# Hybrid two-layer kernel: DMA copies in halves, host-transposed x, 96-row gate matmuls, a new order of gates and outputs

## The chip, the cores and the metric

The kernel runs on one core of a Trainium2 chip. The metric is device time in microseconds, from the start of one execution to its end, median of several runs. The engines are TensorE (PE, with PEld for its weight loads), VectorE (DVE), ScalarE (ACT), GpSimd (POOL) and SyncE (SP), which issues most DMA transfers. Each of them runs its own list of instructions in order, and waits at an instruction until what that needs is there.

## The reference

A sequence of T = 256 tokens of width D = 1024 goes through two layers and a final norm, all in float32:

```python
h = rms_norm(x, norm_w)
proj = h @ w_in
(aq, ak, av, az, c_glu, cz, dq, dk, dvv, dz, db, da, gate_logits) = split(proj)
y_a = diff_attention_branch(aq, ak, av, az, ...)          # 8 heads, two softmaxes each, @ w_attn_out
y_c = conformer_conv_branch(c_glu, cz, ...)               # GLU, depthwise conv of 31 taps, layer norm, @ w_conv_out
y_d = gated_deltanet_branch(dq, dk, dvv, dz, db, da, ...) # below, @ w_dn_out
g_a, g_c, g_d = split(sigmoid(gate_logits), 3)
x = x + (g_a * y_a + g_c * y_c + g_d * y_d) @ w_out
```

The deltanet branch has 8 heads of 128 and works on blocks of time. Per block and head it solves a unit lower triangular system, whose matrix is made of key products and of a decay exp(g_i - g_j), g being a running sum of gates, and then a recurrence over blocks:

```python
g = cumsum(g)
decay = exp(where(causal, g[..., :, None] - g[..., None, :], -inf))
tri = where(strict, einsum('bhnid,bhnjd->bhnij', kb, k) * decay, 0) + eye(C)
sol = triangular_solve(tri, concat([v * beta, kb * exp(g)]), lower=True, unit_diagonal=True)
```

## The kernel before, in words

**Weights.** The weights are read once, as 288 chunks of 512 KB (`w_raw`, `load`, L420-424; three buffers). ACT rounds each chunk to a shorter float type (`w_hi`, a cast) and DVE subtracts (`w_lo`), so that one float32 product becomes three fast matmuls (`acc<-...`, L346): high by high, low by high, high by low. The activations are split likewise (`h_hi`, `h_lo`). Four chunks (two 128-row slices of the 1024 rows each) make a group of 512 output columns: 12 matmuls of 512 columns per chunk, or 24 of 256 where the output is wanted transposed. SP issues the load of chunk n+3 only when the `w_lo` of chunk n is done, since that frees its buffer.

**Order.** Nothing is scheduled by hardware. While the program is built, a planner (class `Stream`) keeps a clock for PE and one for each of ACT, DVE and POOL, and puts the steps of some dozens of generators ("streams") into the gaps beside the dense weight groups. A step is put into its engine's list when the planner's clocks say that its input is there. `dma(landing, ...)` (L353) lists a transfer on SP's queue and tells the planner in how many us it lands; `yield x` in a stream asks for a pause of x us. Once built, the order on each engine is fixed; a wrong guess becomes a wait.

**Stages of a layer.** `SEQ` (L58) is the order of the groups in the first part of a layer: v, k, q are deltanet's projections (0 and 1 are heads 0-3 and 4-7), t the position tables, z the output gates of deltanet, w, x the start of its recurrence with attention's values, c the conformer's projections, a attention's queries and keys, d the depthwise convolution (as matmuls with the shifted copies `u4` and the tap matrices `wd`). Then `PHASE` (L57) orders, for deltanet, conformer and attention, the gate groups (g0, g1, 512 columns of gate logits each) and the output groups (y0, y1, the branch's output times its matrix). `evac_gate` turns gate logits into gate tiles, `evac_y` multiplies them in. Last, w_out.

**Triangular solve** (`dn_keys`, L814 on), once for heads 0-3 and once for heads 4-7 in each layer. PE makes the decay exponents, four heads at a time in `psE`: three bf16 matmuls for each head (the parts `gp[0..2]` of the gates times the triangle `trib`) and one with the causal mask. The 16 x 16 diagonal blocks (`dn_vc`, 128 x 128) are written to device memory (`v_keep`), and one DMA reads them back with a broadcast, so that all partitions of a group of 16 have the same block: 8 source rows, 16 copies of each, 2048 floats per partition, 1 MB in all (`nrep`; `y_hi` for heads 0-3, `t` or `t8` for heads 4-7, after the buffers that it borrows). On these DVE does 15 steps (`dn_t` products, `dn_z` sums), each of which uses the sums before it. The recurrence follows with matmuls on `dn_r`, and its outputs are `o_d`.

**Start.** x is read as 256 KB quarters (`big<-in_x`), two by SP and two by ACT; PE transposes it 128 x 128 at a time into PSUM (`s<-cst,big`), ACT scales and rounds (`h_hi`), DVE takes the rest (`h_lo`), ACT squares for the norm. Eight matmuls on ones (L613) run before.

Of the kernel before, what the change touches and what calls it, by code (L numbers as in the profile page):

```python
# [19 lines left out]
P = 128  # L20
# [36 lines left out]
PHASE = {k: (("g", 0), ("y", 0), ("g", 1), ("y", 1)) for k in ("dn", "conv", "attn")}  # L57
SEQ = "v0 k0 t0 z0 k1 v1 q0 z1 w0 c0 x0 q1 a0 d1 w1 x1 c1 a1 d2".split()  # L58
TAPQ = 8
# [32 lines left out]
def kernel(  # L92
    ctx: ExitStack,
    tc: tile.TileContext,
    x: bass.AP,
    positions: bass.AP,
    wts: bass.AP,
# [109 lines left out]
    def load_x(src):  # L207
        xt = big()
        for q in range(2):
            for t in range(2):  # L210
                qs = slice(q * GW, (q + 1) * GW)
                (nc.sync, nc.scalar if src is x and first_x else nc.sync)[q].dma_start(
                    out=xt[:, t, qs], in_=src[t * P:(t + 1) * P, qs])
        first_x.clear()
        return xt

    first_x = [True]
    u4 = const.tile([P, 8, T], F32, name="u4")
# [3 lines left out]
    one = const.tile([P, 1], F32, name="one")  # L222
    nc.scalar.dma_start(out=cst[:, 0:CO_TRI], in_=consts[:, 0:CO_TRI])
    V.memset(ones, 1.0)
    for i in range(1, 4):
        G.memset(u4[32 * i:32 * i + 32, :, 0:i], 0.0)
    xt = load_x(x)
    S.activation(out=one, in_=ones[:, 0:1], func=AF.Square)
# [8 lines left out]
    pat = const.tile([P, PT_N], BF16, name="pat")  # L237
    trib, identb, mask_dn, mask_at = [pat[:, i * P:(i + 1) * P] for i in range(4)]
    ne16 = cst[:, CO_NE:CO_NE + 16]
# [372 lines left out]
    for _ in range(8):  # L612
        TE.matmul(out=idle[:, 0:P], lhsT=ones, rhs=ones, start=True, stop=True)  # L613
    clk[0] = 4.5
    st_n = start_norm()
    s_r = [(q, add(raw_half(xt, 0, st_n, q))) for q in range(2)]
    finish(s_r[0][1])
    prepare(2)
    prepare()

    for l in range(DEPTH):
# [80 lines left out]
        def ba_stream():  # L702
# [36 lines left out]
            g16 = gg.rearrange("p c h -> p (c h)")
            grem = sm.tile([P, 16], F32, name="grem", bufs=1)  # L740
            V.tensor_copy(out=gp[0], in_=g16)
            V.tensor_sub(out=grem, in0=g16, in1=gp[0])
            V.tensor_copy(out=gp[1], in_=grem)
            V.tensor_sub(out=gp[2], in0=grem, in1=gp[1])
# [784 lines left out]
def _patterns():  # L1529
# [62 lines left out]
```

## Time and profile before

| | us |
|---|---|
| Median of 3 runs | 1125.26 (1125.21 to 1127.08) |
| Profiled execution | 1127.93 |
| Its span in the trace | 1126.1 |
| PE busy | 1055.4 (94%) |
| DVE busy | 864.4 (77%) |
| ACT busy | 550.1 (49%) |

The mean granted clock of PE is 0.964 of full speed. The span is the time between the first and the last event of the trace; the 1.8 us between it and the execution's time lie around it. In the lines of the profile, a time line's row has the start, the duration, the engine, the line of the program, the operation and "output<-inputs"; in square brackets stands how long the engine was idle before it and what released it. A row of waits has the total, the number and the longest. A row of windows has the stretch, its length, the busy time of PE, PEld, DVE, ACT and POOL with the number of instructions, then the granted clock of PE, the share of DMA time and GB/s.

### The profile page before, as it was taken

To read this page: it belongs to the slowest core of one execution; us is meant where nothing else is said; L and a number is where in the kernel's file an instruction comes from. 1 tells how busy PE (TensorE), PEld (TensorE's weight loads), DVE (VectorE), ACT (ScalarE), POOL (GpSimd) and SP (SyncE) were. 2 spreads that over 40 slices of the span, in tenths; PEclk is the share of its full clock that TensorE was granted. 3 is DMA by queue.
4 is the path that set the end of the run, shared out by engine and by line. 5 is a ranking of instruction groups with operands and counts; after the bars stand their busy time and mean duration, and the time that the engine had idled before them with its cause. 6 is when DMAs were issued, how large, how long until landed. Compare 5 with 4: busy or idle time off the path is not lost.

```text
span 1126.1 us, 18152 instructions
## 1 busy us (share of the span) xinstructions
PE 1055.4 (94%) x6964; PEld 915.5 (81%) x6964; DVE 864.4 (77%) x1718; ACT 550.1 (49%) x981; POOL 105.5 (9%) x73
## 2 busy tenths in 40 slices
PE   7998798899999999999999969869999999999996
PEld 6987797689877787898888869758998768879885
DVE  5686887688677899985668869757787689889755
ACT  5663362426445556464465426314544545646543
POOL 0010110010020000121101111011001000011220
PEclk8999898989999999999999989979999999989999
DMA  6556555523634556565664564744354625646662
GB/s 211 155 166 160 161 178 147 128 101 112 181 119 127 181 158 203 174 200 187 198 188 150 167 155 131 224 116 131 95 154 146 168 76 173 197 137 190 199 200 82
DMA packets 57062, 178.07 MB, mean 158 GB/s; under 512 B 6288, under 2 KB 16144, under 8 KB 55696
## 3 DMA queue, kind: packets, MB, share of 16 engines
q1 hardware_dynamic: 55696, 175.43, 51.5%
q10 hardware_dynamic: 1280, 1.49, 0.4%
q8 instruction: 54, 0.88, 0.3%
q14 instruction: 32, 0.26, 0.1%
HBM read 172.44 MB, written 4.46 MB: 157 GB/s over the span
## 4 chain that ended last, share of the span: by engine, by line
PE 79%; DVE 10%; DMA 8%; ACT 1%; issue 1%; SPq 0%; ACTq 0%; DVEq 0%
PE acc L346 65%; PE s L344 11%; DVE w_lo L127 4%; PE s L351 3%; DMA y_hi<-v_keep 2%; DMA t<-v_keep 2%; DMA w_raw<-in_wts 2%; DVE big L127 2%; DMA v_keep<-dn_vc 1%; DVE dn_t L127 1%; ACT w_hi L127 1%; DMA big<-in_x 1%; DVE gx L127 0%; DVE y_lo L127 0%; DVE dn_z L127 0%
## 5 line engine op out<-in xcount | busy, mean ns | idle before, releaser
L127 ACT CAST w_hi<-w_raw 128x1024 fp32r<-128x1024 f32 (+1 forms) x289 | 302.2, 1047 | 363.3 <-PE acc L346 263.4
L127 DVE TENSOR_TENSOR w_lo<-w_raw,w_hi 128x1024 fp32r<-128x1024 f32 (+1 forms) x289 | 369.8, 1280 | 88.0 <-ACT w_hi L127 87.4
L346 PE MATMUL acc<-h_hi,w_lo 128*128 128x256 f32 x768 | 220.0, 286 | 21.0 <-DVE w_lo L127 21.0
L346 PE MATMUL acc<-h_hi,w_hi 128*128 128x256 f32 x768 | 226.9, 295 | 2.8 <-DVE dn_z L127 2.8
L346 PE MATMUL acc<-w_hi,h_hi 128*128 128x512 f32 x512 | 213.1, 416 | 6.6 <-ACT w_hi L127 6.6
L346 PE MATMUL acc<-h_lo,w_hi 128*128 128x256 f32 x768 | 219.3, 286 | 0.0
L346 PE MATMUL acc<-w_lo,h_hi 128*128 128x512 f32 x512 | 202.6, 396 | 1.9 <-DVE w_lo L127 1.9
L346 PE MATMUL acc<-w_hi,h_lo 128*128 128x512 f32 x512 | 202.4, 395 | 0.0
L346 PEld LDWEIGHTS acc<-h_hi,w_lo 128*128 128x128 f32 x768 | 149.1, 194 | 21.6 <-DVE w_lo L127 21.6
L346 PEld LDWEIGHTS acc<-h_hi,w_hi 128*128 128x128 f32 x768 | 149.4, 194 | 5.4 <-issue 4.8
L346 PEld LDWEIGHTS acc<-h_lo,w_hi 128*128 128x128 f32 x768 | 149.3, 194 | 0.5
L346 PEld LDWEIGHTS acc<-w_hi,h_hi 128*128 128x128 f32 x512 | 97.9, 191 | 25.4 <-ACT w_hi L127 7.5
L346 PEld LDWEIGHTS acc<-w_hi,h_lo 128*128 128x128 f32 x512 | 97.5, 190 | 21.4
L346 PEld LDWEIGHTS acc<-w_lo,h_hi 128*128 128x128 f32 x512 | 98.1, 192 | 20.1 <-DVE w_lo L127 3.5
L346 PE MATMUL acc<-w_hi,y_lo 128*128 128x512 f32 x128 | 52.1, 407 | 2.8 <-DVE y_lo L127 2.8
L127 DVE SCALAR_TENSOR_TENSOR c_acc<-c_u,pc,c_acc 128x255 f32<-128x255 f32 (+29 forms) x120 | 52.7, 485 | 2.6 <-ACT c_acc L127 2.6
L346 PE MATMUL acc<-w_hi,y_hi 128*128 128x512 f32 x128 | 53.2, 415 | 0.1
L346 PE MATMUL acc<-w_lo,y_hi 128*128 128x512 f32 x128 | 51.5, 402 | 0.0
L127 POOL TENSOR_TENSOR wa<-wa 128x512 f32<-128x512 f32 x16 | 23.8, 1490 | 281.4 <-DVE wa L127 235.5
L127 DVE SCALAR_TENSOR_TENSOR big<-wc,pc,big 128x255 f32<-128x255 f32 (+2 forms) x96 | 45.9, 519 | 0.0
L127 POOL TENSOR_TENSOR big<-big,gt 128x512 f32<-128x512 f32 x16 | 27.3, 1727 | 181.7 <-DVE gt L127 181.7
L346 PE MATMUL acc<-u,wd 128*32 128x256 f32 (+7 forms) x768 | 41.7, 369 | 1.2 <-ACT c_acc L127 1.2
(261 smaller groups left out, 1544.5 us busy)
## 6 DMA issues: line engine op xcount, KB each, us to landing
w_raw<-in_wts SPq DMA_DIRECT2D x288, 512.0 KB, 3.6
wd<-in_cwd SPq DMA_DIRECT2D x6, 1024.0 KB, 7.3
y_hi<-v_keep SPq DMA_DIRECT2D x2, 1024.0 KB
u_keep<-c_u SPq DMA_DIRECT2D x4, 512.0 KB, 5.2
t<-v_keep SPq DMA_DIRECT2D x2, 1024.0 KB
big<-in_x SPq DMA_DIRECT2D x6, 256.0 KB, 4.8
u<-u_keep SPq DMA_DIRECT2D x6, 256.0 KB, 4.0
u<-u_keep SPq DMA_DIRECT2D x6, 255.0 KB, 5.5
```

Of the source, the lines that this page charges most:

```text
L127: step = (self.key, lambda: getattr(self.eng, op)(*args, **kw), cost)
L344: live[0].steps.append(("PE", lambda: TE.matmul(**kw), cost))
L346: TE.matmul(**kw)
L351: ("PE", lambda: TE.transpose(out=out, in_=in_, identity=ident[0:n, 0:n]), 0.11))
```

## The change

1. x is also given transposed by the host, and layer 0 starts from it: four 256 KB pieces (three on ACT's queue, one on SP's), scaled and split without PE; the first weight chunk is loaded in two halves ahead of them on SP's queue. The squares are summed over rows by ACT and DVE later, and two matmuls of one column sum over partitions. The constants come in three pieces.
2. In `SEQ`, z1 moves from behind q0 to behind c1.
3. `PHASE` of deltanet and attention becomes g0 g1 y0 y1; the gate tiles of g1 come from the pool `wa`.
4. The decay exponents take one matmul per head instead of three: the running sums of the gates are made once per layer as rows (one 96 x 128 matmul), in three bf16 parts on 3 x 32 partitions (`crow`), and a 0/1 pattern `e3` of 96 rows picks the head and adds the parts.
5. The broadcast copy becomes two DMAs of 512 KB; new landings and pauses (3.5, 7.0 with 0.1, 8.0, and 6.0 ahead of the step that first needs the second half) go to the planner.

```diff
-SEQ = "v0 k0 t0 z0 k1 v1 q0 z1 w0 c0 x0 q1 a0 d1 w1 x1 c1 a1 d2".split()
+for k in ('dn', 'attn'):
+    PHASE[k] = (("g", 0), ("g", 1), ("y", 0), ("y", 1))
+SEQ = "v0 k0 t0 z0 k1 v1 q0 w0 c0 x0 q1 a0 d1 w1 x1 c1 z1 a1 d2".split()
...
-    xt = load_x(x)
+    xt = act.tile([P, KT, T], F32, name="big", bufs=3)
+    for k in (0, 2):
+        nc.scalar.dma_start(out=xt[:, k:k + 2], in_=x_t[:, k:k + 2])
...
+    def first_part(k):
+        sc = nwt[:, k:k + 1]
+        xh, xl = st_n["h"]
+        S.activation(out=xh[:, k, :], in_=xt[:, k, :], func=AF.Copy, scale=sc)
+        V.scalar_tensor_tensor(out=xl[:, k, :], in0=xt[:, k, :], scalar=sc, in1=xh[:, k, :].bitcast(F32),
+                               op0=ALU.mult, op1=ALU.subtract)
...
+    load()
+    nc.scalar.dma_start(out=xt[:, 4:6], in_=x_t[:, 4:6])
+    load()
+    nc.sync.dma_start(out=xt[:, 6:8], in_=x_t[:, 6:8])
+    load()
+    nc.scalar.dma_start(out=cst[:, 0:CO_NW], in_=consts[:, 0:CO_NW])
...
-    s_r = [(q, add(raw_half(xt, 0, st_n, q))) for q in range(2)]
-    finish(s_r[0][1])
+    for k in range(2):
+        first_part(k)
     prepare(2)
+    lows(0)
+    for k in range(2, 4):
+        first_part(k)
     prepare()
+    clk[0] = 6.5
+    s_f = add(first_half())
+    s_r = [(1, s_f)]
+    s_q = add(first_squares(), 0.1)
...
+            row = dn_tile()[0:96, 0:P]
+            mm(0.218, out=row, lhsT=gg.rearrange("p n a b -> p (n a b)"), rhs=tri, start=True, stop=True)
...
+            rem = sm.tile([P, P], F32, name="dn_t1", bufs=1)[0:96]
+            mid = sm.tile([96, P], BF16, name="crm", bufs=1)
+            V.tensor_copy(out=crow, in_=row)
+            V.tensor_sub(out=rem, in0=row, in1=crow)
+            V.tensor_copy(out=mid, in_=rem)
+            V.tensor_copy(out=crow[32:64], in_=mid[32:64])
+            V.tensor_sub(out=crow[64:96], in0=rem[64:96], in1=mid[64:96])
...
-                    for n in range(3):
-                        mm(0.055, out=psE[:, h * P:(h + 1) * P], lhsT=gp[n][:, j:j + 1].to_broadcast([P, P]),
-                           rhs=trib, start=(h == 0 and n == 0), stop=False)
+                    mm(0.055, out=psE[:, h * P:(h + 1) * P], lhsT=e3[:, j:j + 1].to_broadcast([96, P]),
+                       rhs=crow, start=(h == 0), stop=False)
...
-            dma(2.5, out=v_keep[hs], in_=vc.rearrange("p c h i -> p (c h i)"))
-            dma(
-                6.0, out=nrep.rearrange("p j c i -> p (j c i)"),
-                in_=v_keep[hs].rearrange("(b j) n -> b (j n)", b=8).unsqueeze(1).to_broadcast([8, 16, 16 * P]))
-            yield
+            dma(3.5, out=v_keep[hs], in_=vc.rearrange("p c h i -> p (c h i)"))
+            yield 3.5
+            for half in range(2):
+                dma(0.1 if half else 7.0, out=nrep[:, 8 * half:8 * half + 8].rearrange("p j c i -> p (j c i)"),
+                    in_=v_keep[hs].rearrange("(b h j) n -> h b (j n)", b=8, h=2)[half].unsqueeze(1).to_broadcast(
+                        [8, 16, 8 * P]))
+            yield 8.0
             z = sm.tile([P, 8, 16], F32, name="dn_z", bufs=1)
             V.tensor_copy(out=z, in_=bc_mid(eye16, 8))
...
-                if i % 3 == 0:
-                    yield
+                if i % 3 == 0 or i == 7:
+                    yield 6.0 if i == 7 else None
...
-                        g = flat(gt())
+                        g = flat(wa() if i else gt())
```

Two places show how the order moves. The first is SP's queue at the block copy of layer 0, heads 0-3 (`v_keep` written from `dn_vc`, then read back with the broadcast into `y_hi`). Before:

```order
L423 DMA w_raw<-in_wts 128x1024 x28
L354 DMA v_keep_85<-dn_vc 128x128
L354 DMA y_hi<-v_keep_85 128x1x2048
L423 DMA w_raw<-in_wts 128x1024 x15
L354 DMA u_keep<-c_u 128x4x256
```

After the change:

```order
L427 DMA w_raw<-in_wts 128x1024 x30
L357 DMA v_keep_85<-dn_vc 128x128
L427 DMA w_raw<-in_wts 128x1024 x4
L357 DMA y_hi<-v_keep_85 128x1x1024 x2
L427 DMA w_raw<-in_wts 128x1024 x4
L357 DMA u_keep<-c_u 128x4x256
```

Four weight loads moved between the write and the read, and the read is two DMAs, issued one right after the other.

The second place is DVE's list at the start of the solve on those blocks (`dn_z` set from the constants, then products `dn_t` and sums `dn_z`). Before:

```order
L127 COPY dn_z<-cst 128x128
L127 TENSOR_TENSOR w_lo<-w_raw,w_hi 128x1024
L127 TENSOR_TENSOR dn_t_1104<-dn_z,y_hi 128x8x2
L127 TENSOR_REDUCE dn_z<-dn_t_1104 128x8
L127 TENSOR_TENSOR dn_t_1105<-dn_z,y_hi 128x8x3
L127 TENSOR_REDUCE dn_z<-dn_t_1105 128x8
L127 TENSOR_TENSOR dn_t_1106<-dn_z,y_hi 128x8x4
L127 TENSOR_TENSOR w_lo<-w_raw,w_hi 128x1024
```

After the change:

```order
L130 TENSOR_TENSOR w_lo<-w_raw,w_hi 128x1024
L130 SCALAR_TENSOR_TENSOR vv<-wc,pc,vv 128x253
L130 COPY dn_z<-cst 128x128
L130 TENSOR_TENSOR dn_t_1372<-dn_z,y_hi 128x8x2
L130 TENSOR_REDUCE dn_z<-dn_t_1372 128x8
L130 TENSOR_TENSOR dn_t_1373<-dn_z,y_hi 128x8x3
L130 TENSOR_REDUCE dn_z<-dn_t_1373 128x8
L130 TENSOR_TENSOR dn_t_1374<-dn_z,y_hi 128x8x4
L130 TENSOR_REDUCE dn_z<-dn_t_1374 128x8
L130 TENSOR_TENSOR w_lo<-w_raw,w_hi 128x1024
```

The first read of `y_hi` stands behind a split of weights in both, one operation later than before; that split is the one which frees the buffer for the last of the four weight loads above (chunk 34 of 288, whose buffer chunk 37 takes). The next split follows after three steps of the solve.

More of the change, by code (lines that the diff above doesn't have):

```diff
@@ L95 @@
     x: bass.AP,
+    x_t: bass.AP,
     positions: bass.AP,
@@ L211, in load_x @@
                 qs = slice(q * GW, (q + 1) * GW)
-                (nc.sync, nc.scalar if src is x and first_x else nc.sync)[q].dma_start(
-                    out=xt[:, t, qs], in_=src[t * P:(t + 1) * P, qs])
-        first_x.clear()
+                nc.sync.dma_start(out=xt[:, t, qs], in_=src[t * P:(t + 1) * P, qs])
         return xt
-    first_x = [True]
     u4 = const.tile([P, 8, T], F32, name="u4")
@@ L222 @@
     one = const.tile([P, 1], F32, name="one")
-    nc.scalar.dma_start(out=cst[:, 0:CO_TRI], in_=consts[:, 0:CO_TRI])
+    nc.scalar.dma_start(out=cst[:, CO_NW:CO_TRI], in_=consts[:, CO_NW:CO_TRI])
     V.memset(ones, 1.0)
@@ L237 @@
     pat = const.tile([P, PT_N], BF16, name="pat")
-    trib, identb, mask_dn, mask_at = [pat[:, i * P:(i + 1) * P] for i in range(4)]
+    e3 = pat[0:96, 0:16]
+    identb, mask_dn, mask_at = [pat[:, i * P:(i + 1) * P] for i in range(1, 4)]
     ne16 = cst[:, CO_NE:CO_NE + 16]
@@ L422, in load @@
             raw = wpool.tile([P, KC, GW], F32, name="w_raw", bufs=RAW)
-            nc.sync.dma_start(out=raw, in_=wts[queue[len(raws)]])
+            for kk in range(KC) if not raws else [slice(0, KC)]:
+                nc.sync.dma_start(out=raw[:, kk], in_=wts[queue[len(raws)]][:, kk])
             raws.append((raw, clk[0] + 4.5))
@@ L604, in raw_half, with first_half, first_squares @@
             square_half(xt, st["ss"], q, t)
-    for _ in range(RAW):
-        load()
+    def first_part(k):
[4 more added lines that the diff above has]
+                               op0=ALU.mult, op1=ALU.subtract)
+    def first_half():
+        yield 1.5
+        for k in range(4, KT):
+            first_part(k)
+            yield
+    def first_squares():
+        yield from until(s_f)
+        sums = wc()[:, 0, :]
+        for q in range(2):
+            sq = wa().rearrange("p (a b) d -> p a (b d)", a=2)
+            sq2 = wa().rearrange("p (a b) d -> p a (b d)", a=2)
+            for n, s in enumerate((sq, sq2)):
+                S.activation(out=s, in_=xt[:, 4 * q + 2 * n:4 * q + 2 * n + 2, :], func=AF.Square)
+            yield
+            V.tensor_tensor(out=sq, in0=sq, in1=sq2, op=ALU.add)
+            V.tensor_tensor(out=sq[:, 0], in0=sq[:, 0], in1=sq[:, 1], op=ALU.add)
+            if q:
+                V.tensor_tensor(out=sums, in0=sums, in1=sq[:, 0], op=ALU.add)
+            else:
+                V.tensor_copy(out=sums, in_=sq[:, 0])
+            yield
+        pss = side_tile()
+        for t in range(2):
+            mm(0.218, out=pss[:, t:t + 1], lhsT=sums[:, t * P:(t + 1) * P], rhs=ones[:, 0:1],
+               start=(t == 0), stop=(t == 1))
+        ms = sm.tile([P, 2], F32, name="nms", bufs=2)
+        V.tensor_scalar(out=ms, in0=pss[:, 0:2], scalar1=1.0 / D, scalar2=1e-6, op0=ALU.mult, op1=ALU.add)
+        st_n["rn"] = rsqrt(ms, 2, "n")
+    load()
[4 more added lines that the diff above has]
+    nc.scalar.dma_start(out=cst[:, 0:CO_NW], in_=consts[:, 0:CO_NW])
     nc.scalar.dma_start(out=cst[:, CO_TRI:CO_N], in_=consts[:, CO_TRI:CO_N])
@@ L613 @@
         TE.matmul(out=idle[:, 0:P], lhsT=ones, rhs=ones, start=True, stop=True)
-    clk[0] = 4.5
+    clk[0] = 5.0
     st_n = start_norm()
-    s_r = [(q, add(raw_half(xt, 0, st_n, q))) for q in range(2)]
-    finish(s_r[0][1])
+    for k in range(2):
+        first_part(k)
     prepare(2)
+    lows(0)
+    for k in range(2, 4):
+        first_part(k)
     prepare()
+    clk[0] = 6.5
+    s_f = add(first_half())
+    s_r = [(1, s_f)]
+    s_q = add(first_squares(), 0.1)
     for l in range(DEPTH):
@@ L640 @@
         beta = lay.tile([P, 2, 8], F32, name="beta")
-        gg = lay.tile([P, 2, 8], F32, name="gg")
+        gg = lay.tile([P, 3, 2, 16], F32, name="gg")
         ng = lay.tile([P, 16], F32, name="ng")
@@ L679, in norm_stream @@
         def norm_stream():
-            yield from until(s_r[1][1])
-            st_n["rn"] = rn = inv_rms(st_n["ss"])
+            if l == 0:
+                yield from until(s_q)
+                rn = st_n["rn"]
+            else:
+                yield from until(s_r[1][1])
+                st_n["rn"] = rn = inv_rms(st_n["ss"])
             dgt = wa()
@@ L735, in ba_stream @@
             V.scalar_tensor_tensor(out=zl, in0=za, scalar=0.0, in1=zl, op0=ALU.max, op1=ALU.add)
-            V.scalar_tensor_tensor(out=gg, in0=zl, scalar=-1.0, in1=bc_mid(ea, 2), op0=ALU.mult, op1=ALU.mult)
+            V.memset(gg, 0.0)
+            g16 = gg[:, 0].rearrange("p a b -> p (a b)")[:, 0:16]
+            V.scalar_tensor_tensor(out=g16.rearrange("p (c h) -> p c h", c=2), in0=zl, scalar=-1.0,
+                                   in1=bc_mid(ea, 2), op0=ALU.mult, op1=ALU.mult)
+            V.tensor_copy(out=gg.rearrange("p n a b -> p n (a b)")[:, 1:3, 0:16], in_=bc_mid(g16, 2))
             yield
             psg = dn_tile()
[L739 to L744, printed above, removed]
             mm(0.218, out=psg[:, 0:16], lhsT=tri, rhs=g16, start=True, stop=False)
             mm(0.218, out=psg[:, 16:32], lhsT=ones, rhs=g16, start=False, stop=True)
+            row = dn_tile()[0:96, 0:P]
+            mm(0.218, out=row, lhsT=gg.rearrange("p n a b -> p (n a b)"), rhs=tri, start=True, stop=True)
             V.tensor_scalar(out=ng, in0=psg[:, 0:16], scalar1=-1.0, scalar2=None, op0=ALU.mult)
@@ L761, in evac_v @@
             return f
-        finish(s_r[0][1])
+        if l:
+            finish(s_r[0][1])
         s_norm = add(norm_stream(), 0.1)
@@ L810, in apply4 @@
             return pm
-        gp = [sm.tile([P, 16], BF16, name=f"gp{n}", bufs=1) for n in range(3)]
+        crow = lay.tile([96, P], BF16, name="crow")
         def dn_keys(hs, st):
@@ L1533, in _patterns @@
     c = np.zeros((P, PT_N), f)
-    c[:, 0:P] = p[:, None] <= p[None, :]
+    c[:, 0:16] = (p[:, None] % 32) == np.arange(16)[None, :]
     c[:, P:2 * P] = np.eye(P, dtype=f)
@@ L1576 @@
     arrays = {
-        "x": a["x"].reshape(T, D), "positions": a["positions"], "wts": wts, "wba": wba, "cwd": cwd,
+        "x": a["x"].reshape(T, D),
+        "x_t": a["x"].reshape(T, KT, P).transpose(2, 1, 0), "positions": a["positions"], "wts": wts, "wba": wba, "cwd": cwd,
         "pch": pch, "prow": prow,
```

## The prediction

> **What bounds the kernel now.** I read the page first (engines, slices), then the waits of PE and of DVE, then the time line of each long wait with the DMA of that stretch. The page's engine line:
>
> ```profile
> span 1126.1 us, 18152 instructions
> PE 1055.4 (94%) x6964; PEld 915.5 (81%) x6964; DVE 864.4 (77%) x1718; ACT 550.1 (49%) x981; POOL 105.5 (9%) x73
> ```
>
> TensorE (PE) has work 94% of the span, so the end moves in only two ways: PE waits less than 1126.1 - 1055.4 = 70.7 us, or it gets less work. The waits of PE, and of DVE (total, times, longest):
>
> ```profile
> PE acc L346 <- DVE w_lo L127: 22.9, 6, 10.5
> PE s L344 <- DVE dn_r L127: 16.5, 3, 10.6
> PE acc L346 <- DVE y_lo L127: 2.8, 2, 1.9
> PE s L351 <- DVE o_d L127: 1.9, 3, 1.1
> DVE dn_t L127 <- DMA y_hi<-v_keep: 25.0, 2, 13.0
> DVE dn_t L127 <- DMA t<-v_keep: 22.9, 2, 12.5
> ```
>
> Four waits of DVE for the block copy (y_hi or t from v_keep, 47.9 us together) stand behind PE's long ones. Here is the first (layer 0, heads 0-3):
>
> ```profile
> 99.58 0.43 SPq L354 DMA_DIRECT2D v_keep<-dn_vc  x1
> 102.54 1.22 DVE L127 TENSOR_TENSOR w_lo<-w_raw,w_hi 128x1024 fp32r<-128x1024 f32 x1
> 103.09 0.73 SPq L354 DMA_DIRECT2D y_hi<-v_keep  x1
> 116.77 0.19 DVE L127 TENSOR_TENSOR dn_t<-dn_z,y_hi 128x16 f32<-128x16 f32 x1 [13.01 <-DMA y_hi<-v_keep]
> 117.78 1.22 DVE L127 TENSOR_TENSOR w_lo<-w_raw,w_hi 128x1024 fp32r<-128x1024 f32 x1
> 119.05 0.58 PE L346 MATMUL acc<-h_hi,w_lo 128*128 128x256 f32 x1 [10.26 <-DVE w_lo L127]
> ```
>
> The copy lands 116.77 - 103.09 = 13.7 us after its issue. DVE works in order, so the next weight split (w_lo) is stuck behind the waiting read. PE had 13.01 + (119.05 - 116.77) - 10.26 = 5.0 us of work in hand and then stood still. After such a wait the granted clock is low too:
>
> ```profile
> 118.00:124.00 6.00, 4.95 (x23) 4.95 (x24) 5.76 (x14) 2.04 (x3) 0.00 (x0) 0.51 0.54 159
> ```
>
> A clock of 0.51 over 4.95 busy us costs another 2.4. [...]
>
> **The change part by part.** *Block copies.* SP no longer sits between v_keep and the copy; three or four weight loads stand there, and the copy goes in two halves. But the order puts DVE's first read of half 1 right behind the w_lo that frees the buffer of the last load ahead of it, so DVE again waits for a whole landing, now of one half. What does a half take? DMA shares in 40 slices of 98 to 120 us, and the same in GB/s:
>
> ```profile
> DMA  9302958710136299998995999564455344554001
> GB/s 380 142 0 22 179 223 341 264 44 0 30 60 89 89 201 179 223 194 149 194 171 74 186 216 171 75 112 104 134 119 112 67 112 171 201 216 186 7 0 7
> ```
>
> From about 111 us the copy is alone and keeps 4 to 5 tenths of the DMA engines busy. Size does not scale this away: v_keep, a sixteenth of the copy's bytes, lands 103.09 - 99.58 = 3.5 us after issue. With 3.3 fixed, a half takes 3.3 + 10.4/2 = 8.5, and 512 KB of weights issued just ahead go first: at the 341 of the row 1.5 us. So half 1 lands some 10.2 us after that w_lo ends, against 13.0 before. Bounds: 6.9 (half of 13.7, nothing fixed) and 13.7. I take 10.2, which is nearest to what the rows add up to. [...] Half 2 is read four or five weight chunks later and costs nothing, since 4 chunks of PE work (about 10.9 us, below) cover its 5.2.
>
> What hides 10.2 us? The 5.0 in hand, as before. The four places:
>
> ```profile
> 225.00 0.36 PE L346 MATMUL acc<-h_hi,w_hi 128*128 128x256 f32 x1 [2.81 <-DVE dn_z L127]
> 236.68 0.58 PE L344 MATMUL s<-dn_r,t 128*128 128x128 f32 x1 [2.60 <-DVE dn_r L127]
> 657.08 0.19 DVE L127 TENSOR_TENSOR dn_t<-dn_z,y_hi 128x16 f32<-128x16 f32 x1 [12.00 <-DMA y_hi<-v_keep]
> 660.07 0.58 PE L346 MATMUL acc<-h_hi,w_lo 128*128 128x256 f32 x1 [10.49 <-DVE w_lo L127]
> 751.97 2.07 PE L344 MATMUL s<-dn_r,dn_vo 128*128 128x128 f32 x8 [10.60 <-DVE dn_r L127]
> ```
>
> Layer 0, heads 0-3: 10.2 + 2.5 (three solve steps, 117.78 - 116.77 and a bit, then the split of 1.22) - 5.0 = 7.7 instead of 10.26: -2.6. Layer 1, heads 0-3: five steps now stand ahead of the next w_lo, as long as the 3.0 from 657.08 to 660.07 and 0.7 more: 10.2 + 3.7 - 4.7 = 9.2 instead of 10.49: -1.3. Layer 0, heads 4-7: today the depthwise matmuls hide most of the copy (2.81 + 2.60 are left). The change puts the solve among the conformer's projections, ahead of d2, and that cover is gone: 10.2 + 3.2 - 4.9 = 8.5, so +3.1. Layer 1, heads 4-7: 10.60 becomes 10.2 + about 3.5 (more steps, y_lo) - 4.9 = 8.8: -1.8. Sum -2.6; with less half clock behind the two shortened pairs I take -4. Bounds: -14 (landing 6.9) to +8 (landing 13.7 and no work in hand for heads 4-7).
>
> *SP behind u_keep.* In layer 1 SP stood on u_keep's landing, then w_raw came late:
>
> ```profile
> 709.80 0.44 SPq L354 DMA_DIRECT2D u_keep<-c_u  x1
> 710.29 0.50 SPq L354 DMA_DIRECT2D wd<-in_cwd  x1
> 715.26 1.93 SPq L354 DMA_DIRECT2D u<-u_keep  x4
> 727.75 0.56 PE L346 MATMUL acc<-w_hi,h_hi 128*128 128x512 f32 x1 [2.76 <-ACT w_hi L127]
> 729.01 0.80 PE L346 MATMUL acc<-w_lo,h_hi 128*128 128x512 f32 x1 [0.70 <-DVE w_lo L127]
> 729.00:735.00 6.00, 5.99 (x20) 5.22 (x21) 5.66 (x18) 1.39 (x2) 0.00 (x0) 0.51 0.47 146
> ```
>
> 715.26 - 709.80 = 5.5 us without a weight load, then 3.46 us of idle PE and 6 us at clock 0.51 (2.9 lost). The new order has a w_raw between u_keep and wd, so the stretch shrinks by one issue. Worth 0 to -6.4; I take -4.5.
>
> *Start.* Before (PE's transposes, h_hi, casts, first product):
>
> ```profile
> 5.62 0.39 ACTq L610 DMA_DIRECT2D pos_i<-in_positions  x1
> 7.90 2.61 PE L351 MATMUL s<-cst,big 128*128 128x128 f32 x11 [1.85 <-DMA big<-in_x]
> 8.83 2.55 ACT L127 ACTIVATE h_hi<-s,cst 128x256 fp32r<-128x256 f32 x6 [1.94 <-PE s L351]
> 13.72 3.02 ACT L127 CAST w_hi<-w_raw 128x512 fp32r<-128x512 f32 x4
> 14.38 0.79 PE L346 MATMUL acc<-w_hi,h_hi 128*128 128x512 f32 x1 [3.87 <-ACT w_hi L127]
> ```
>
> Now two h_hi and half a cast come ahead of the first product, on x as it lands: no transposes, and the squares move behind. ACT issues its pos_i load only when the second x piece is down (5.62 before; 5.6 to 7.9 now, 7.9 being the row of the last piece of x), then 2 x 2.55/6 = 0.85 and 3.02/4 = 0.75, and a hop: first product at 7.3 to 9.6, I take 8.0. That is -6.4; the two small matmuls of the norm give 0.4 back: -6.0, bounds -4.4 and -6.7. The squares, sums and low parts lie on ACT (49%) and DVE in the first 20 us, beside PE's first group.
>
> *Gate rows.* Twelve matmuls per block of four heads become four; before:
>
> ```profile
> 66.81 0.84 PE L344 MATMUL s<-pat,gp 128*128 128x128 bf16 x12
> 67.49 0.38 PE L344 MATMUL s<-pat 128*128 128x512 bf16 x1
> ```
>
> 67.49 - 66.81 = 0.68 for 12, 0.057 each. Two layers, two head sets, two blocks of time: eight such groups, 64 fewer matmuls, -3.6. The extra row matmul and the DVE operations (some 0.2 us each, like dn_t's 0.19, five more per layer) stand at the start of a layer, where PE has dense weight work in hand; if that cover failed it would be +1 per layer.
>
> *Phases g0 g1 y0 y1.* In layer 1 the first outputs wait for their inputs, deltanet's for o_d (1.9 in three waits, quoted above) just before 909 us and attention's for y_lo at 994.93:
>
> ```profile
> 909.00:913.00 4.00, 4.00 (x14) 3.15 (x13) 3.93 (x13) 0.59 (x2) 0.00 (x0) 0.58 0.02 4
> 994.93 0.79 PE L346 MATMUL acc<-w_hi,y_lo 128*128 128x512 f32 x1 [1.86 <-DVE y_lo L127]
> 998.00:1002.00 4.00, 4.00 (x12) 3.08 (x11) 1.28 (x2) 1.58 (x2) 0.00 (x0) 0.61 0.00 0
> 27.28 0.39 PE L346 MATMUL acc<-w_lo,h_hi 128*128 128x512 f32 x1
> 27.51 0.39 PE L346 MATMUL acc<-w_hi,h_lo 128*128 128x512 f32 x1
> ```
>
> A gate group ahead of y0 is 4 chunks of 12 products, 0.23 apart (the last two rows): 10.9 us for DVE to finish in. Waits of 1.9 and 1.9 go, with 4 x 0.42 = 1.7 and 4 x 0.39 = 1.6 of clock, and 0.9 that is left of y_lo's 2.8 in layer 0: at most -8.0. I take -6; it is 0 if the second gate tiles, now from another pool, hold up something else. z1's later place moves dense work only: 0.
>
> Sum: -4 - 4.5 - 6.0 - 3.6 - 6 = -24. The profiled execution took 1127.93 us (span 1126.1 and 1.8 around it), 2.7 above the median of 1125.26. Against the median: 1101 us.
>
> **The rivals.**
> 1. *The copies are hidden after all*: half 1 is down when DVE gets there. For it: v_keep's wait is gone, and a few loads more lie in between. Against: read and issue hang on the same w_lo. Remaining waits 10.26 + 10.49 + 10.60 + 5.4 = 36.7 go, with 2.4 of clock at three of them, instead of the 4 above: 1101 - 40 = 1061. It decides if DVE's waits for the copies sum to under 10 us.
> 2. *The change doesn't do what it says for the copies*: the pause meant for the landing moves the issue itself, and half 1, behind weights, comes as late as the whole (13.7). Then 3.5 more at each of four places, and half the phase and u_keep gains with it as the waits only wander: 1101 + 14 + 5 = 1120; with the other gains intact 1115.
> 3. *Slower*: for heads 4-7 the solve and the recurrence of heads 0-3 (dn_r) share DVE, and PE's next step hangs on dn_r. If the copy, all 15 steps and the recurrence run one after the other there (13.7, 15 steps at the 0.4 of 116.77 to 117.78, and four trips like the 2.60 above: 30), each layer stands 30 - 9 = 21 longer than forecast: 1101 + 42 = 1143. It decides from 12 us more per layer. Against it: chunks' splits stand between the steps in the order.
>
> **How the numbers follow.** Forecast 0.63, rival 1 0.09, rival 2 0.19, rival 3 0.09. Forecast's own ends: -14 and +8 of the copies, the u_keep and phase terms between full and none give 1087 to 1116. The range reaches down past this toward rival 1 and up over most of rival 2: 1084 to 1121. About 0.2%, 2.3 us, is what a measurement of this kernel can tell from no change. Faster: 0.63 + 0.09 + 0.15 = 0.87; same 0.03, the top of rival 2; slower 0.10.
>
> **What would show it.** Right: first product near 8 us; DVE's waits for the halves near 10 us each (7 for layer 0, heads 4-7), the w_raw ahead of them early; PE waits of 7 to 9 at four places; no w_hi wait after u_keep; no o_d or y_lo waits. Wrong: waits for the copies under 3 us, or a new releaser with over 10 us, first of all dn_r.

## The result, and the profile after

The changed kernel takes 1117.51 us (median of 4 runs, 1114.95 to 1120.10), the kernel before in the same measurement 1126.17: ratio 0.9921, 95% interval 0.9893 to 0.9949. It is faster by 8.7 us; the prediction said 24 (1101 us, range 1084 to 1121). The time lies in the range, the gain is a third of the forecast. The profiled execution took 1114.95 us, 12.98 less than the one before (1127.93).

The head of the page of the changed kernel:

```profile
span 1113.2 us, 18028 instructions
PE 1044.5 (94%) x6892; PEld 905.1 (81%) x6892; DVE 866.7 (78%) x1729; ACT 548.3 (49%) x977; POOL 102.3 (9%) x73
```

PE is idle for 1113.2 - 1044.5 = 68.7 us, against 70.7 before. So nearly all of the gain in this execution is busy time (1055.4 - 1044.5 = 10.9), and the waits have only changed places. Most of the busy time that went was work: PE's transposes of x (in the profile's groups `s<-cst,big` falls from 18.7 to 14.8 us) and the gate rows (`s<-pat,gp`, 6.8 us, became `s<-crow,pat`, 3.2). The rest goes with the clock, whose mean is 0.971 instead of 0.964. How the waits changed places, the waits of PE and of DVE say (total, times, longest):

```profile
PE acc L349 <- DVE w_lo L130: 14.7, 6, 6.7
PE s L354 <- POOL t L130: 11.7, 1, 11.7
PE s L347 <- DVE y_lo L130: 8.3, 2, 4.3
PE s L347 <- DVE gf L130: 6.3, 2, 3.5
DVE dn_t L130 <- DMA y_hi<-v_keep: 17.0, 2, 8.7
DVE dn_t L130 <- DMA t<-v_keep: 11.7, 2, 6.0
```

DVE waits 28.7 us for the copies instead of 47.9. The row `s <- POOL t` is new, and it is PE's longest wait. Two stretches of the time line belong to these rows. The first is the block copy of layer 0, heads 0-3:

```profile
109.12 0.42 SPq L357 DMA_DIRECT2D v_keep<-dn_vc  x1
119.79 1.35 SPq L357 DMA_DIRECT2D y_hi<-v_keep  x2
128.66 0.19 DVE L130 TENSOR_TENSOR dn_t<-dn_z,y_hi 128x16 f32<-128x16 f32 x1 [8.75 <-DMA y_hi<-v_keep]
131.17 0.58 PE L349 MATMUL acc<-h_hi,w_lo 128*128 128x256 f32 x1 [6.69 <-DVE w_lo L130]
```

The halves are issued 119.79 - 109.12 = 10.7 us behind the write of v_keep. Half 1 lands 128.66 - 119.79 = 8.9 us after its issue, and the reader arrives at once: DVE stands 8.75 us, PE 6.69. The second stretch comes 20 us later, where SP copies the conformer's activations:

```profile
139.23 0.43 SPq L357 DMA_DIRECT2D u_keep<-c_u  x1
139.71 0.51 SPq L357 DMA_DIRECT2D wd<-in_cwd  x1
144.53 2.16 SPq L357 DMA_DIRECT2D u<-u_keep  x4
146.79 0.40 SPq L427 DMA_DIRECT2D w_raw<-in_wts  x1
157.85 1.04 ACT L130 CAST w_hi<-w_raw 128x1024 fp32r<-128x1024 f32 x1 [12.03 <-DMA w_raw<-in_wts]
161.55 2.41 POOL L130 TENSOR_TENSOR t<-dn_z,cst 128x512 f32<-128x512 f32 x2 [68.34 <-DVE dn_z L130]
162.82 1.12 PE L354 MATMUL s<-cst,t 128*128 128x128 f32 x4 [11.65 <-POOL t L130]
169.27 1.01 PE L347 MATMUL s<-dn_vo,gf 128*128 128x128 f32 x3 [2.77 <-DVE gf L130]
```

No weights are requested from 139.2 to 146.8, then 2 MB (tap matrices and shifted copies) are ahead of them, and the chunk is there at 157.85, 11 us after its issue. ACT stands 12.03 us. Its cast is followed on DVE by the split, and behind that split lie the last two steps of the solve, which POOL's `t` and so PE's next matmul need. That is why the releaser reads POOL, an engine that had nothing to do with the cause. The granted clock of the stretch, with the fields of a window (length, busy PE, PEld, DVE, ACT, POOL, clock, DMA share, GB/s):

```profile
150.00:176.00 26.00, 11.57 (x40) 8.97 (x39) 13.80 (x24) 8.77 (x15) 2.41 (x2) 0.61 0.41 115
```

In 26 us PE is busy for 11.57, and that mostly at half clock (0.61 in the mean). Before the change the same copies also came without a load of weights between them (160.57 to 168.59), and the chunk behind them was there 9.7 us after its issue (178.31), but PE had products in hand until 182.9 us and waited only 3.3 (the rest of dn_r's 16.5 beside the 10.6 and 2.6 that the prediction quotes).

The start, in which ACT's wait for the DMAs shows:

```profile
9.38 0.39 ACTq L655 DMA_DIRECT2D pos_i<-in_positions  x1
9.82 0.91 ACT L130 ACTIVATE h_hi<-big,cst 128x256 fp32r<-128x256 f32 x2 [6.17 <-DMA big<-in_x_t]
11.29 0.80 PE L349 MATMUL acc<-w_hi,h_hi 128*128 128x512 f32 x1 [6.59 <-ACT w_hi L130]
```

The first product comes at 11.29 (14.38 before, 8.0 forecast).

### The profile page after: what moved, and what is told of

It is laid out like the page before. It is cut to its first block, busy times and chain, and to the rows that moved or that the text cites. A ratio compares the mean times of both kernels' runs of the same rounds, so it can differ in the third digit from the quotient of the medians.

```text
span 1113.2 us, 18028 instructions
## 1 busy us (share of the span) xinstructions
PE 1044.5 (94%) x6892; PEld 905.1 (81%) x6892; DVE 866.7 (78%) x1729; ACT 548.3 (49%) x977; POOL 102.3 (9%) x73
## 4 chain that ended last, share of the span: by engine, by line
PE 69%; DVE 17%; DMA 8%; issue 3%; ACT 2%; SPq 0%; ACTq 0%; DVEq 0%
PE acc L349 55%; PE s L347 11%; DVE w_lo L130 6%; DMA w_raw<-in_wts 4%; PE s L354 3%; DVE big L130 2%; DMA y_hi<-v_keep 1%; DMA t<-v_keep 1%; ACT w_hi L130 1%; DVE c_acc L130 1%; DVE vv L130 1%; DVE gx L130 1%; DMA big<-in_x_t 1%; DVE dn_t L130 1%; DMA u_keep<-c_u 0%
## 5 line engine op out<-in xcount | busy, mean ns | idle before, releaser
L130 DVE TENSOR_TENSOR w_lo<-w_raw,w_hi 128x1024 fp32r<-128x1024 f32 (+1 forms) x289 | 365.5, 1266 | 77.7 <-ACT w_hi L130 76.8
L349 PE MATMUL acc<-h_hi,w_hi 128*128 128x256 f32 x768 | 224.5, 292 | 0.0
L349 PE MATMUL acc<-w_hi,h_hi 128*128 128x512 f32 x512 | 216.0, 422 | 6.6 <-ACT w_hi L130 6.6
L349 PE MATMUL acc<-w_hi,t 128*128 128x512 f32 x128 | 40.0, 389 | 0.0
L349 PEld LDWEIGHTS acc<-u,wd 128*32 128x32 f32 x768 | 23.7, 110 | 18.3 <-ACT c_acc L130 3.5
```

The costliest lines, as they stand in the source:

```text
L130: step = (self.key, lambda: getattr(self.eng, op)(*args, **kw), cost)
L349: TE.matmul(**kw)
```

## The experiments

"Ratio" is to the kernel before, measured beside each kernel on the same chip, with its 95% interval. Three chips were used (e1 to e4, e5 to e8, e9 to e12), so kernels of different groups are best compared by their ratios.

| kernel | us | ratio |
|---|---|---|
| the change | 1117.51 | 0.9921 [0.9893, 0.9949] |
| e1 the change, z1 back | 1114.04 | 0.9891 [0.9872, 0.9911] |
| e2 the change, tap matrices earlier | 1110.82 | 0.9856 [0.9832, 0.9880] |
| e3 the change, halves issued early, read late | 1091.69 | 0.9686 [0.9662, 0.9710] |
| e4 the change, constants behind first scalings | 1112.37 | 0.9867 [0.9846, 0.9888] |
| e5 the change, old phases | 1117.56 | 0.9943 [0.9921, 0.9965] |
| e6 e3 with 16 source rows | 1080.82 | 0.9606 [0.9588, 0.9624] |
| e7 e6 with e4's start | 1079.84 | 0.9594 [0.9575, 0.9613] |
| e8 before, halves alone | 1120.63 | 0.9959 [0.9946, 0.9971] |
| e9 before, start and gate rows alone | 1131.08 | 1.0061 [1.0043, 1.0079] |
| e10 before, 16 source rows alone | 1104.22 | 0.9830 [0.9808, 0.9851] |
| e11 e7 with tap matrices far ahead | 1070.92 | 0.9528 [0.9508, 0.9548] |
| e12 before, halves and new phases | 1114.22 | 0.9920 [0.9898, 0.9941] |

**e1: z1 back behind q0.**

```diff
-SEQ = "v0 k0 t0 z0 k1 v1 q0 w0 c0 x0 q1 a0 d1 w1 x1 c1 z1 a1 d2".split()
+SEQ = "v0 k0 t0 z0 k1 v1 q0 z1 w0 c0 x0 q1 a0 d1 w1 x1 c1 a1 d2".split()
```

> The changed kernel with z1 back behind q0, nothing else. Theory A: what ate the gain is the wait of 11.7 us at 162.8 us and the half clock up to 175 us in layer 0, because z1's move brought u_keep, the tap matrices and the shifted copies (2.5 MB in one burst) to a place where only two weight chunks were ready. With z1 back u_keep comes four chunks later with a weight load behind it, that wait goes, and 10 to 18 us of the changed kernel's time with it: 1100 to 1108. Rival B: z1's place is neutral, as the prediction had it, and the wait at 162.8 us is the late end of the triangular solve, which is late here too: 1114 to 1120, the wait still there.

The wait at 162.8 us is gone, as A has it, and the time fell by only about 3 us, near B's end. SP's queue with z1 back:

```profile
149.64 0.43 SPq L357 DMA_DIRECT2D u_keep<-c_u  x1
152.05 0.34 SPq L427 DMA_DIRECT2D w_raw<-in_wts  x1
152.45 0.45 SPq L357 DMA_DIRECT2D wd<-in_cwd  x1
```

One load of weights goes between, and no PE wait over 0.5 us follows from 131 to 235 us. But others appear, in PE's waits of the same kernel:

```profile
PE s L354 <- ACT gx L130: 6.1, 1, 6.1
PE s L354 <- DVE big L130: 4.4, 2, 4.0
```

The recurrence of heads 4-7 (gx at 268 us) and attention's output (big at 987 us) now wait. PE's idle time falls from 68.7 to 1110.3 - 1050.0 = 60.3 us, but its busy time, for as many matmuls, rises from 1044.5 to 1050.0: part of the gain is lost in slower products. A's mechanism holds and its price doesn't: z1's four chunks of dense work hide something wherever they stand, and moving them bares something else.

**e2: tap matrices earlier.**

```diff
+            if s == 0 and NV < 2:
+                s_cv[NV] = add(conv_load(NV))
             s_g = group_a(l, ("in", CG + s * GW), H, evac_g)
...
-                if s == 0 and NV < 2:
-                    s_cv[NV] = add(conv_load(NV))
```

> The changed kernel with the 1 MB of tap matrices loaded ahead of the conformer's first group (nine loads of weights sooner in layer 0) and no longer between u_keep and the shifted copies; order of DVE and PE unchanged. Theory A (the burst holds back weight chunk 42): the chunk lands some 2.5 to 5 us sooner, the wait at 162.8 us falls from 11.7 to 6 to 9, time 1109 to 1114. Rival B (the solve ends late by itself): wait and time unchanged, 1115 to 1119.

ACT's and PE's rows at the same place:

```profile
152.48 1.04 ACT L130 CAST w_hi<-w_raw 128x1024 fp32r<-128x1024 f32 x1 [5.56 <-DMA w_raw<-in_wts]
157.45 0.90 PE L354 MATMUL s<-cst,t 128*128 128x128 f32 x3 [5.19 <-POOL t L130]
```

With 1 MB less ahead of it the chunk is there 152.48 - 146.27 = 6.2 us after its issue instead of 11.1, and PE's wait falls from 11.65 to 5.19. The order on DVE and PE is the same, so the burst, not a late solve, sets this wait; A stands, its time (1109 to 1114) too. How long it is varies with the execution (7.2 us in e4's, 9.8 in e5's, which leave the burst alone).

**e3: halves issued early, read placed behind the landing.**

```diff
             dma(3.5, out=v_keep[hs], in_=vc.rearrange("p c h i -> p (c h i)"))
-            yield 3.5
+            yield
             for half in range(2):
-                dma(0.1 if half else 7.0, out=nrep[:, 8 * half:8 * half + 8].rearrange("p j c i -> p (j c i)"),
+                dma(9.0 if half else 0.1, out=nrep[:, 8 * half:8 * half + 8].rearrange("p j c i -> p (j c i)"),
...
-            yield 8.0
+            yield 3.5
```

> The changed kernel with the pauses where they act: the halves are issued 3.5 us after the write of v_keep instead of 11.5, and DVE's first step of the solve is placed 9 us behind their issue. Theory C (in the changed kernel the 8.0 pause holds back the issue of the halves instead of the read): DVE's waits for the copies fall from 28.7 us to under 6, PE's four waits behind them (6.7, 4.0, 6.5, 4.3) go, and with the half clock behind them 20 to 30 us: 1088 to 1098. Rival D (the halves share the DMA engines with the weight loads, so whatever is not waited for at the copy is waited for at the next weight chunk): waits move to the casts and splits of weights, 1108 to 1117.

The issue of the first copy, then PE's and DVE's waits:

```profile
107.42 0.43 SPq L357 DMA_DIRECT2D v_keep<-dn_vc  x1
113.64 1.74 SPq L357 DMA_DIRECT2D y_hi<-v_keep  x2
PE acc L349 <- ACT w_hi L130: 15.6, 3, 6.0
PE acc L349 <- DVE w_lo L130: 3.2, 6, 0.9
DVE dn_t L130 <- DMA y_hi<-v_keep: 3.8, 2, 2.3
DVE dn_t L130 <- DMA t<-v_keep: 0.4, 1, 0.4
```

C holds. A pause given by `yield` is added to the planner's time before the steps just listed are placed, so the change's 8.0 held back the copies themselves, in the planner's time 3.5 + 8.0 = 11.5 us behind v_keep, while the read followed the issue at once. By the same rule the `yield 3.5` left in e3 puts the halves 7.0 us behind v_keep and not 3.5, as was expected. In the traces they come 5.1 to 9.2 us behind it at the four places (here 113.64 - 107.42 = 6.2), in the changed kernel 10.5 to 11.2. With that, and the read placed 9 us behind the issue, the waits for the copies fall from 28.7 to 4.2 us, and about 25 us go. Not all of that is the copies': the new order also puts a load of weights between u_keep and the tap matrices (at 141.12 us), and PE's wait for POOL's `t` is 1.8 us instead of 11.7. D is there too, but small: of the 15.6 us for casts, 4.7 (at 130.0 us) and 4.8 (at 656.6) are weight loads stuck behind the copies.

**e4: constants behind the first scalings.** The four loads of `cst`, `cst`, `pat` and `pos_i` on ACT's queue stand behind `prepare(2)` and `lows(0)`.

> The changed kernel with the four loads of constants, patterns and positions on ACT's queue moved behind the first two scalings and the first cast. Theory E (ACT stands at the issue of these loads while the first two pieces of x are there): scaling starts at 7.4 us instead of 9.8, the first product at 9 instead of 11.3, 2 to 2.5 us faster than the changed kernel: 1114 to 1116. Rival F (x or the first half of the weights lands that late): first product at 11 to 11.5, time unchanged.

```profile
7.04 0.51 ACT L130 ACTIVATE h_hi<-big,cst 128x256 fp32r<-128x256 f32 x1 [3.38 <-DMA big<-in_x_t]
8.50 0.50 PE L349 MATMUL acc<-w_hi,h_hi 128*128 128x512 f32 x1 [3.66 <-ACT w_hi L130]
```

E holds: the first piece of x was there at 7.0, ACT stood at an issue that waited for another piece (pos_i, at 9.38 in the changed kernel). The first product gains 11.29 - 8.50 = 2.8; the time gains 5, more than E said, and a shorter wait at 157.9 us (7.2 instead of 11.7 in the profiled executions) is large enough for the rest.

**e5: old phases.**

```diff
-for k in ('dn', 'attn'):
-    PHASE[k] = (("g", 0), ("g", 1), ("y", 0), ("y", 1))
...
-                        g = flat(wa() if i else gt())
+                        g = flat(gt())
```

> The changed kernel with the phases of deltanet and attention back at g0 y0 g1 y1 and the second gate tiles back in their pool. Theory H (the prediction's term): the new order of phases is worth 6 us, so this kernel takes 1122 to 1126, with waits for o_d and y_lo at layer 1's outputs of about 3.8 us and half clock behind them. Rival I: only the waits for o_d (1.9) and layer 0's y_lo (0.9) went with it, since attention's wait of 1.9 for y_lo at 995.6 us is still there in the changed kernel: 2 to 4 us, 1118.5 to 1121.5.

1117.56 against 1117.51: by the medians neither H nor I, and the phases are worth nothing here. By the ratios (0.9943 against 0.9921) they are worth 2.5 us, with intervals that overlap, so I isn't excluded. H's waits did not come back: PE waits 0.6 us for o_d and 1.0 for y_lo at the outputs. With z1 behind c1 there are four more chunks between the solve and deltanet's outputs, which would explain why o_d is ready in the old order too; that was not tried by itself.

**e6: 16 source rows**, on e3. The blocks are written twice, one copy behind the other for each group:

```diff
-            dma(3.5, out=v_keep[hs], in_=vc.rearrange("p c h i -> p (c h i)"))
+            for c in range(2):
+                dma(3.5 if c else 0.1, out=v_keep[hs].rearrange("(b c j) n -> c b j n", b=8, c=2)[c],
+                    in_=vc.rearrange("p c h i -> p (c h i)"))
...
-                    in_=v_keep[hs].rearrange("(b h j) n -> h b (j n)", b=8, h=2)[half].unsqueeze(1).to_broadcast(
-                        [8, 16, 8 * P]))
+                    in_=v_keep[hs].rearrange("(a h j) n -> h a (j n)", a=16, h=2)[half].unsqueeze(1).to_broadcast(
+                        [16, 8, 8 * P]))
```

> The kernel with the halves issued early (1091.7), and the blocks written twice to device memory, so that the broadcast copy reads 16 rows with 8 copies of each instead of 8 rows with 16. Theory J (with 8 source rows a copy runs on eight of the sixteen DMA engines, and what is left of its cost is the weight load queued behind it there): on sixteen it takes about half as long, DVE's waits of 4.2 us go, and PE's waits for the cast at 130.0 and 656.6 us (4.7 and 4.8) shrink below 2.5: 1082 to 1088. Rival K (the copy is bound by its bytes or by the 4 KB pieces, not by the number of rows): 1090 to 1094, the waits for the cast as before.

The two places where e3 waited for the cast, first in e3, then here:

```profile
130.00 0.58 PE L349 MATMUL acc<-h_hi,w_hi 128*128 128x256 f32 x1 [4.73 <-ACT w_hi L130]
656.57 0.58 PE L349 MATMUL acc<-h_hi,w_hi 128*128 128x256 f32 x1 [4.84 <-ACT w_hi L130]
127.27 0.39 PE L349 MATMUL acc<-h_hi,w_hi 128*128 128x256 f32 x1 [0.73 <-ACT w_hi L130]
647.77 0.39 PE L349 MATMUL acc<-h_hi,w_lo 128*128 128x256 f32 x1 [0.76 <-DVE w_lo L130]
```

4.73 and 4.84 became 0.73 and 0.76, DVE's waits for the copies 1.6 instead of 4.2; J holds, with 1.2 us more than its range, and the ratios' intervals don't touch.

**e7: 16 rows and e4's start.**

> The same with 16 rows, and with the loads of constants behind the first scalings as well: all that helped, together. If the two gains stand apart (another stage, other waits), 2.5 to 5 us below the kernel with 16 rows alone; if the start's gain is given back at the next wait for weights or for the norm, under 1 us.

1079.84 against 1080.82: no gain that can be told from none. The first product is at 9.46 in its profile (10.82 in e6's), so the 2.8 of e4 is the upper end of what this order of loads gives.

**e8: halves alone.** The change's copy, pauses and step 7's pause in the kernel before.

> The kernel before with the copy in halves and its pauses alone; start, order of groups, phases and gate rows as before. Theory L (the copies are the largest gain of the change, hidden by the other parts' losses): the four waits fall from 36.8 to about 20 us, and half clock with them: 15 to 22 us faster than before, 1105 to 1112. Rival M (the prediction's term): 2 to 6 us faster than before, 1121 to 1125.

The four waits behind the copies fell from 36.8 to 4.2 + 3.5 + 4.2 + 6.1 = 18.0 us, and the kernel is only 4.8 us faster, within M's 2 to 6. Much of the reason stands in PE's time line:

```profile
352.19 1.17 PE L351 MATMUL s<-cst,o_d 128*128 128x128 f32 x4 [5.35 <-DVE o_d L127]
904.82 0.45 PE L351 MATMUL s<-cst,o_d 128*128 128x128 f32 x1 [7.49 <-DVE o_d L127]
```

The solve for heads 4-7 ends later: its last sum comes at 264.2 us in layer 0 and 793.8 in layer 1, before at 236.1 and 776.1. In layer 0 half of that is the later start (235.8 instead of 222.0) and half the longer run (28 us instead of 14), in which the new pause of 6.0 ahead of step 7 stands; which of copy and pause does how much was not tried. So 12.8 us are given back at deltanet's outputs. L's first half is right, its sum wrong.

**e9: start and gate rows alone.** The change with `SEQ`, phases, gate tiles and copy as before.

> The kernel before with the new start and the new gate rows, the rest (copy, order of groups, phases) as before. Theory P (terms read off the changed kernel's trace: first product 3.1 us sooner, 2.8 given back at the norm, gates 3.6): 2 to 6 us faster than before, 1120 to 1124. Rival Q (the prediction's two terms, 6.0 and 3.6): 8 to 11 us faster, 1114.5 to 1117.5.

Slower than before, by 0.4 to 0.8%; both theories fell. The copy of layer 0, heads 4-7, on SP, DVE and PE:

```profile
218.36 0.61 SPq L355 DMA_DIRECT2D t<-v_keep  x1
230.40 0.19 DVE L128 TENSOR_TENSOR dn_t<-dn_z,t 128x16 f32<-128x16 f32 x1 [12.39 <-DMA t<-v_keep]
232.14 2.08 PE L345 MATMUL s<-gx 128*128 128x128 f32 x8 [11.15 <-DVE gx L128]
```

The planner's clock had moved by a few us, v_keep came three chunks later in the order, and the depthwise matmuls that had hidden this copy before (2.81 + 2.60 us left) no longer stood beside it: 11.15. PE's waits for o_d grew too, from 1.9 to 6.4 us. Which of the two parts moved the copy was not tried.

**e10: 16 source rows alone**, whole copy, kernel before.

> The kernel before with one difference: the blocks are written twice and the whole 1 MB copy reads 16 rows with 8 copies of each. If the number of source rows sets how many DMA engines a copy runs on (theory J), the copy lands 7.5 to 9 us after its issue instead of 13.7, DVE's waits fall from 47.9 to about 27 us, PE's four waits from 36.8 to about 17, and with the half clock 18 to 26 us go: 1099 to 1108. If the gain of the 16-row kernel came from somewhere else: landing 13 to 14 us, time 1124 to 1128.

```profile
105.42 0.60 SPq L354 DMA_DIRECT2D y_hi<-v_keep  x1
112.65 0.18 DVE L127 TENSOR_TENSOR dn_t<-dn_z,y_hi 128x16 f32<-128x16 f32 x1 [7.24 <-DMA y_hi<-v_keep]
114.93 0.58 PE L346 MATMUL acc<-h_hi,w_lo 128*128 128x256 f32 x1 [4.50 <-DVE w_lo L127]
```

The whole 1 MB lands 7.2 us after its issue instead of 13.7, sooner than half of it did in the change (8.9, behind a weight load). DVE's waits are 13.4 + 12.9 = 26.3. DMA shares of 98 to 116 us in 40 slices:

```profile
DMA  1927950089576441100969998899859899981009
```

From about 107 to 112 us they stand mostly at 8 to 9 tenths (weight loads among it), where the copy alone ran at 4 to 5 before. The time is in the range that goes with J. These 21 us, without halves, are more than twice what the whole change brought.

**e11: tap matrices far ahead**, on e7 (`conv_load` started at k1).

> All that helped so far (16 rows, halves issued early, constants behind the first scalings), and the tap matrices loaded in deltanet's projections, far from u_keep. Theory A (what is left at 146 to 157 us and at 676 us is the burst of tap matrices and shifted copies ahead of a weight chunk): the waits there (3.3, 4.9 and 4.1) fall by more than half, 6 to 10 us off the kernel without it: 1069 to 1074. Rival R (they come from the length of DVE's work there, or the 1 MB shared copies alone): 1077 to 1081.

1070.92 us, in A's range, 54 us or 4.7% faster than the kernel before. A holds in layer 1, where the wait of 4.1 at 676 us is gone. In layer 0 it holds only in part: waits of 3.2 and 3.1 are left of 3.3 and 4.9. DVE is busy without a gap there from 130 to 150 us, so the first of them hangs on the length of DVE's work, as R had it. PE is busy 1035.6 of 1070.1 us.

**e12: halves and new phases.**

> The kernel before with the halves and their pauses, and the new order of phases; no other part. Theory N (with the halves the solve ends later, and the kernel then waits 13.0 us for o_d at deltanet's first outputs; a second gate group ahead of them covers that): these waits fall under 2 us, 1107 to 1114. Rival S (no order of phases helps, as undoing it in the changed kernel cost nothing): 1118 to 1122.

1114.22, just outside N's range and clear of S's: 6.4 less than e8, with intervals of the ratios that don't overlap. The waits for o_d fell from 13.0 to 8.3 in all (5.35 to 1.73 in layer 0, 7.49 to 5.79 in layer 1). The phases do pay where the solve ends late and z1 stands early, though a second gate group does not cover all of it.

## Why the prediction was right or wrong

The forecast was -24 us, and -8.7 came. The steps that failed are z1's term (0), the start (-6.0), the phases (-6, by e5's medians) and u_keep (-4.5); the copies gave more than their -4, and only the gate rows came as forecast.

- **Block copies: mechanism right, size too small.** Half 1 landed 8.9, 8.0, 7.9 and 7.3 us after its issue where my sum has 8.5 + 1.5 = 10.0 (119.79 to 128.66; 236.16 to 244.13; 660.74 to 668.64; 770.62 to 777.87). The four waits of PE fell to 6.69 + 4.03 + 6.52 + 4.31 = 21.6 us; I had -2.6 of idle time, and it was -15.2. For heads 4-7 I took the next split as what PE waits for. It was y_lo, which stands right behind the first read:

```profile
245.18 1.22 PE L347 MATMUL s<-big 128*128 128x128 f32 x4 [4.03 <-DVE y_lo L130]
```

- **"z1's later place moves dense work only: 0" failed.** I looked at what z1's chunks contain and not at what their place leaves bare. Without them u_keep and its 2 MB came where two chunks were ready, and PE's work in hand ended at 151.2 us, 6.7 us before the next chunk was there: 14.4 us of waits for 3.3, and 26 us at clock 0.61. At that place this is about as much as the copies gained. What z1's move costs in all is less: with z1 back (e1) other waits come up, and only some 3 us go. I had read this very pattern in layer 1 and priced its end at -4.5, and did not ask layer 0's order for it.
- **u_keep in layer 1: 0 instead of -4.5.** Behind the first u_keep the wait for w_hi is gone and 1.89 us for ACT's `t` are left (704.87 us, at a clock of 1.00 from 700 to 712) of 3.46; 3.55 came behind the second u_keep, which my term leaves out:

```profile
818.20 1.20 PE L347 MATMUL s<-dn_vo,gf 128*128 128x128 f32 x4 [3.55 <-DVE gf L130]
```

- **Start: -0.3 instead of -6.0.** The step that failed is the landing of the second piece of x, which I took from before (5.6 us); with three weight requests now issued beside it, it was down at 9.4 (the last increment of its semaphore comes at 9.36 us, the issue of pos_i at 9.38), and ACT, which had to issue pos_i behind that, could not scale the first piece that was there at 7.0 (e4). That the weights delay x was not tried by itself. And the norm that I priced at 0.4 waits 2.77 for its sums on DVE:

```profile
29.67 0.49 PE L347 MATMUL s<-ones,wc 128*128 128x1 f32 x3 [2.77 <-DVE wc L130]
```

- **Gate rows: right.** The four matmuls now take 74.07 - 73.83 = 0.24 us up to the mask's instead of 0.68, at all eight places: -3.5.

```profile
73.83 0.40 PE L347 MATMUL s<-crow,pat 96*128 96x128 bf16 x4
74.07 0.38 PE L347 MATMUL s<-pat 128*128 128x512 bf16 x1
```

- **Phases: 0 instead of -6, by e5's medians.** The step that failed is that a gate group ahead of y0 gives DVE 10.9 us to finish in. For deltanet's o_d the same time was already there in the old order (e5), it seems by z1's new place; with z1 early and the solve late the phases do pay (e12). For attention DVE made y_lo only at 994.11 to 995.52 us, in spite of the gate group ahead, and the wait was not touched at all:

```profile
995.57 0.50 PE L349 MATMUL acc<-w_hi,y_lo 128*128 128x512 f32 x1 [1.96 <-DVE y_lo L130]
```

- **The rivals.** Rival 1 was wrong for this change (28.7 us of waits for the copies against a bound of 10). With the copies issued earlier its mechanism came (e3, 4.2 us of waits), though not its 1061 us. Its 2.4 us of clock at each of three places was an estimate from one of them; behind the other two, at 660.07 and 751.97 us in the kernel before, the clock was 0.74 (660 to 666) and 0.72 (752 to 758), 1.5 and 1.7 us of PE's busy time there. Rival 2 named the true defect, that the pause moves the issue. The measured 1117.5 lies in its 1115 to 1120, but by luck: half 1 landed in 8.9 us at most, not 13.7, and what took the time was elsewhere. Rival 3 did not come.
- **The range.** The forecast's own upper end of 1116 is not the sum of its terms: +12 for the copies, +4.5 for u_keep and +6 for the phases on 1101 give 1123. That the result lies in the range is not to the credit of the mechanism. A smaller slip: the work in hand of 4.7 and 4.9 us is 4.5 in layer 1 (12.00 + 660.07 - 657.08 - 10.49).

Behind single terms stands one error: I added terms that were each worked out in the old order. The parts share their covers. Halves alone give 4.8 us, halves and phases 11, phases alone in the new order none, start and gate rows alone lose 6. What stays open: z1's own worth (e1 gains 3 us on the change, with intervals that overlap), that of the phases in the changed kernel to some us, and which part of e9 moved the copy.

## What to carry to other kernels

In a program whose order is planned, a moved block of dense work is a moved cover: list for each queue what stands beside it now, and beside its old place, before calling it free. When a releaser is an engine that had nothing to do, follow the chain to the transfer behind it; here POOL's name stood for a burst of 2 MB on SP's queue. And before a slow transfer is cut or hidden, ask why it is slow: eight source rows became sixteen, and the copy took 7.2 us instead of 13.7.

## What the runs showed of the hardware

The number of source rows of this copy set how much of the DMA engines it used: the same 1 MB, in 8 rows read 16 times each, took 13.7 us with the engines at 4 to 5 tenths (the kernel before), and in 16 rows read 8 times each 7.2 us, with the engines mostly at 8 to 9 tenths (e10, weight loads among it). The traces show it in the landing too: the semaphore of each 8-row copy, the counter by which its landing is told, gets its last eight increments 12.6 to 13.7 us after the issue (the kernel before, where each write of v_keep gets sixteen, at 2.7 to 3.7 us); the four 16-row copies land 6.8 to 7.3 us after theirs (e10). No other number of rows was run for this copy.

Attention's wait for y_lo was followed by a low clock before the change (1.86 us at 994.93, then 0.61 from 998 to 1002) and by full clock after it (1.96 us at 995.57):

```profile
993.00:1001.00 8.00, 6.04 (x26) 4.68 (x27) 6.57 (x9) 3.35 (x6) 0.00 (x0) 1.00 0.35 123
```

So a wait of under 2 us stood ahead of half clock in one kernel and of full clock in the other. What decides it, no run here isolates.
